# The second part of split weights, made by an accumulating DMA in place of a VectorE subtraction

## The chip, the cores and the metric

The kernel runs on one core of a Trainium2 chip. The metric is the device time of one execution in microseconds (us). A core has TensorE (PE in the profile, with its weight loads as PEld), VectorE (DVE), ScalarE (ACT), GpSimd (POOL), the SyncE queue (SP), and 16 DMA engines that move data for every queue that issues a DMA.

## The reference

Two layers of a diffusion backbone over 256 latent tokens `x` and 256 context tokens `ctx`, of 1024 channels each, all in float32. In each layer the same weights serve both streams:

```python
for layer in range(DEPTH):                       # DEPTH = 2
    x = x + 0.5 * mx[2] * swiglu(modulate(rms_norm(x), mx[0], mx[1]), ffn1_w_gu[layer], ffn1_w_down[layer])
    ctx = ctx + ...                              # the same, with mc and the same weights
    hx = modulate(rms_norm(x), mx[3], mx[4])     # attention, pooling and Fourier groups from hx @ w_in
    x = x + mx[5] * merge_mixers(...)            # ... @ w_out
    x = x + 0.5 * mx[8] * swiglu(modulate(rms_norm(x), mx[6], mx[7]), ffn2_w_gu[layer], ffn2_w_down[layer])
    if not last:                                 # ctx goes through mixer and second block in layer 0 alone
        ctx = ctx + ...
return rms_norm(x) * final_gain
# swiglu: g, u = split(h @ w_gu); (silu(g) * u) @ w_down, with 2816 hidden channels
# mx, mc = silu(c) @ ada_w[layer] + ada_b[layer], in nine parts of 1024
```

## The kernel before

Every large product is made exact to float32 by splitting both operands in two float32r parts, a rounded one and the rest. `mm3` then issues three matmuls for each 128 by 128 piece of a weight: rounded by rounded (L394), rounded weight by rest of the activation (L395), rest of the weight by rounded activation (L396). The input projection of the mixer does the same in L926 to L928.

The weights come through a `Feeder`. It holds a fixed plan: blocks of 1 MB in the order of their use, each loaded by one DMA of the SP queue (L160; the output projection's blocks by three) into one of three `raw` buffers. A block is used in two halves of 128 by 1024 values (512 KB), 300 halves in all. `split()` writes the rounded part of a half with ScalarE (L193), into a fresh tile `a`. `flush()` then writes the rest into a second tile with VectorE: `raw` minus rounded (L171). When both halves of a block have been flushed, its raw buffer is given back and `load()` issues the next block's DMA. So the DMA of block n+3 waits for the second subtraction of block n.

All of this is one straight program. `Sched` adds up an estimate of TensorE's time while the program is written, and side work is put between the matmuls when that estimate reaches its due time: `tick()` calls `split()` at least 1500 ns after the last one and `flush()` 1100 ns after its copy, unless the plan is held (`hold`) or six to eight halves (`limit`; two in attention) are split and not yet used up. `get()` splits at once where a half is needed and isn't there. The queues of the engines are in order, so what the program writes is what each engine does, and only its waits depend on time.

Two other streams share the queues. `ada_stream` loads the modulation weights in blocks of 512 KB by the SP queue (L568) and multiplies them on VectorE (L589, L591). The residual is updated on VectorE (L704), and gates and products of the feed-forward run on ScalarE (L662, L669) and VectorE (L667, L672). GpSimd has a memset of a small tile in each layer (L808) and no DMA.

In the first feed-forward blocks and layer 0 both streams go through the matmuls together (512 columns); the last feed-forward block, from about 1435 us on, has the latent stream alone (256 columns), so that each half of a weight serves half as much TensorE work.

Of the kernel before, what the change touches and what calls it, by code (L numbers as in the profile page):

```python
# [10 lines left out]
F32 = mybir.dt.float32  # L11
# [36 lines left out]

# Constants that depend on the shapes alone.
def _tables():  # L50
# [34 lines left out]
class Sched:  # L85
    """Places side work among the tensor engine's main stream by an estimate of its time."""

# [43 lines left out]
class Feeder:  # L131
    """Streams weight blocks in the order of their use and splits them into two exact float32r parts."""

# [32 lines left out]
    def flush(self):  # L166
        if self.part is None:
            return
        b, key, vh, vl, src = self.part
        self.part = None  # L170
        self.nc.vector.tensor_sub(vl, src, vh.bitcast(F32))  # L171
        self.live[key] = (vh, vl)
        b["left"] -= 1
        if b["left"] == 0:
            del self.raw[b["name"]]
            self.raw_live -= 1
            self.load()

    def split(self):
        self.flush()  # L180
        self.load()
        if self.n_split >= len(self.plan) or self.half_live >= self.limit:
            return False
        name, h = self.plan[self.n_split]
        if name not in self.raw:
            return False
        b = self.blocks[self.index[name]]
        src = b["halves"][h](self.raw[name])
        i = self.n_split
        view = (lambda t: t.rearrange("p (a b) -> p a b", a=src.shape[1])) if len(src.shape) == 3 else (lambda t: t[:, :])  # L190
        vh = view(self.tile(F32R))
        vl = view(self.tile(F32R))
        self.nc.scalar.copy(vh, src)  # L193
        self.part = (b, (name, h), vh, vl, src)
        self.half_live += 1
        self.n_split += 1
        self.next = self.S.t + SPLIT_GAP
        return True
# [31 lines left out]
def tile_hybrid_dit(  # L230
# [39 lines left out]

# [1 line left out]
    small = cst.tile([P, 802], F32, name="small", tag="small")  # L272
# [22 lines left out]

# [1 line left out]
    first_raw = {}  # L297
# [90 lines left out]

# [1 line left out]
    def mod(l, m, d, s):  # L390
# [10 lines left out]

# [1 line left out]
    def load_rows(l):  # L403
# [114 lines left out]

# [1 line left out]
    ada_ok = set()  # L520
# [10 lines left out]
    def ada_start(p):  # L531
        """Shift and scale of the first block for the channels p * 256 ..., on the tensor engine."""
        ps = psum()
        for m in range(2):
            for k in range(KD):
                raw = first_raw[p, m, k // 4][:, k % 4, :]
                j = k % 4
                mm(  # L538
                    ps[32 * j:32 * j + 32, m * 256:(m + 1) * 256], c32[:, k, :], raw,
                    start=(k < 4), stop=(k >= 4),  # L540
                )
            S.pe(900)
        sbt = t2()
        nc.vector.tensor_copy(sbt, ps)
        yield 600
        tp = psum()
        for i in range(4):
            mm(tp[:, 2 * i:2 * i + 2], sbt[:, i * P:(i + 1) * P], sel, start=True, stop=True)
        S.pe(1600)
        for m in range(2):  # L550
            c0 = m * 8 + p * 2
            nc.vector.tensor_tensor(
                out=modT[0][:, c0:c0 + 2, :], in0=tp[:, 4 * m:4 * m + 4].rearrange("p (i s) -> p i s", i=2),
                in1=vecT[0][:, c0:c0 + 2].unsqueeze(2).to_broadcast([P, 2, 2]), op=ALU.add,
            )
            mod_fix(0, m, c0, c0 + 2)
        ada_ok.add((0, "start", p))
# [82 lines left out]

# [1 line left out]
    def ffn(l, w, streams, h_tasks, tail, early=None):  # L642
# [142 lines left out]
    class Tail:  # L785
        """Collects squares of the new residual and starts the next normalization."""

# [13 lines left out]

# [1 line left out]
    def load_mix_consts(l):  # L803
# [16 lines left out]
    def qk_norm(src, nh, which, T):  # L820
        """RMS-norms the heads in src [128 tokens, nh, 64] (PSUM), with gain and rope; returns float32."""
        sq = t2()
# [32 lines left out]
    def mix(l, h_tasks, tail):  # L855
# [98 lines left out]

        # pooling and Fourier groups, the tensor engine's work between the steps of attention
        def pool_fft():
# [38 lines left out]
            def do_f2(s, _):  # L995
                # The real part for the frequencies 129 .. 255 mirrors that of 127 .. 1.
                ps = psum()
# [74 lines left out]

        # attention
        def attend(Ts, k0, nkc, per_unit, fill_ns):
# [93 lines left out]

        # output projection
        need_ada(l, 5)  # L1170
# [34 lines left out]

# [1 line left out]
    rows0 = load_rows(0)  # L1207
# [123 lines left out]

# [1 line left out]
    class End:  # L1333
# [76 lines left out]
```

## Time and profile before

| | |
|---|---|
| device time, median of two runs | 1625.3 us (1624.01 and 1626.58) |
| span of the profiled execution, first to last instruction | 1621.4 us, 3.9 us under that median |
| TensorE busy | 1599.8 us, 99% |
| VectorE busy | 1147.4 us, 71% |
| ScalarE busy | 589.5 us, 36% |
| GpSimd busy | 0.8 us |
| DMA engines' mean busy share, SP's queue | 44.5% |

Busy times are of one profiled execution, of which the profile gives the span and no other time of its own. An engine's share is over the whole span; the stages differ, and a table by stage stands among the rows below. A DMA packet's time counts on the one of the 16 engines that moves it, so a share of 44.5% is the mean over the 16.

### The profile page before, as it was taken

What the parts mean: (1) busy time and instruction counts of PE and PEld (TensorE: products, weight loads), DVE (VectorE), ACT (ScalarE), POOL (GpSimd) and SP (SyncE); (2) the same over time, 40 slices, a digit from 0 to 9 for tenths busy, and PEclk for the clock granted to TensorE, in tenths of its full rate; (3) what the DMA queues carried; (4) which work ended last, traced back from release to release, by engine and by line L of the source; (5) the groups of instructions that cost most, each with busy time, mean ns of one, the idle gap of its engine ahead of it and who ended that gap; (6) DMA issues with size and microseconds to landing.
All of it is one profiled execution on the core that took longest, in us unless ns stands there. A gap on an engine that the chain in (4) does not pass through costs nothing.

```text
span 1621.4 us, 22361 instructions
## 1 busy us (share of the span) xinstructions
PE 1599.8 (99%) x9039; PEld 1362.1 (84%) x9039; DVE 1147.4 (71%) x1959; ACT 589.5 (36%) x963; POOL 0.8 (0%) x6
## 2 busy tenths in 40 slices
PE   7999999999999999999999999999999999999998
PEld 5888888888886998888888898888888897899998
DVE  4788888886857567656644677888887587665556
ACT  4422232133557442222222352222232356654343
POOL 0000000000000000000000000000000000000000
PEclk9999999999999999999999999999999999999999
DMA  9756465553022335434432324555464323445452
GB/s 331 241 190 198 152 222 194 171 193 104 33 53 53 130 108 180 151 130 153 144 107 83 125 100 162 183 192 193 145 221 144 113 88 79 131 156 182 157 184 77
DMA packets 165590, 241.28 MB, mean 149 GB/s; under 512 B 6468, under 2 KB 115696, under 8 KB 165232
## 3 DMA queue, kind: packets, MB, share of 16 engines
q1 hardware_dynamic: 163536, 238.99, 44.5%
q8 instruction: 71, 1.16, 0.3%
q10 hardware_dynamic: 1952, 0.87, 0.2%
q14 instruction: 31, 0.25, 0.0%
HBM read 238.79 MB, written 1.05 MB: 148 GB/s over the span
## 4 chain that ended last, share of the span: by engine, by line
PE 97%; DVE 2%; ACT 1%; DMA 0%; issue 0%; SPq 0%; DVEq 0%
PE ps L394 28%; PE ps L395 28%; PE ps L396 27%; PE ps L926 2%; PE ps L928 2%; PE ps L927 2%; PE ps L1136 1%; PE ps L1113 1%; PE ps L603 1%; PE ps L1085 0%; PE ps L538 0%; PE ps L474 0%; PE ps L610 0%; PE ps L1086 0%; PE ps L484 0%; PE ps L902 0%
## 5 line engine op out<-in xcount | busy, mean ns | idle before, releaser
L394 PE MATMUL ps<-ahi,a 128*128 128x512 f32 (+1 forms) x1664 | 581.7, 350 | 1.7 <-ACT ahi L494 1.1
L395 PE MATMUL ps<-alo,a 128*128 128x512 f32 (+1 forms) x1664 | 578.4, 348 | 1.3 <-DVE alo L498 1.3
L396 PE MATMUL ps<-ahi,a 128*128 128x512 f32 (+1 forms) x1664 | 577.9, 347 | 1.5 <-DVE a L171 1.5
L171 DVE TENSOR_TENSOR a<-raw,a 128x1024 fp32r<-128x1024 f32 x300 | 363.5, 1222 | 138.2 <-ACT a L193 137.7
L394 PEld LDWEIGHTS ps<-ahi,a 128*128 128x128 f32 x1664 | 316.5, 190 | 51.5 <-issue 10.8
L193 ACT CAST a<-raw 128x1024 fp32r<-128x1024 f32 x300 | 304.8, 1044 | 150.2 <-PE ps L395 94.3
L396 PEld LDWEIGHTS ps<-ahi,a 128*128 128x128 f32 x1664 | 316.5, 190 | 41.0 <-DVE a L171 1.9
L395 PEld LDWEIGHTS ps<-alo,a 128*128 128x128 f32 x1664 | 316.6, 190 | 40.7 <-DVE alo L498 2.7
L591 DVE SCALAR_TENSOR_TENSOR a<-ada,c,a 128x512 f32<-128x512 f32 x448 | 320.6, 746 | 21.8 <-DMA ada<-in_ada_w_dram 21.2
L394 PE MATMUL ps<-a,a 128*128 128x512 f32 (+1 forms) x800 | 273.8, 342 | 0.0
L396 PE MATMUL ps<-a,a 128*128 128x512 f32 (+1 forms) x800 | 272.3, 340 | 0.0
L395 PE MATMUL ps<-a,a 128*128 128x512 f32 (+1 forms) x800 | 272.2, 340 | 0.0
L704 DVE SCALAR_TENSOR_TENSOR xT<-ps,modT,xT 128x256 f32<-128x256 f32 x336 | 149.2, 479 | 78.9 <-PE ps L396 78.5
L394 PEld LDWEIGHTS ps<-a,a 128*128 128x128 f32 x800 | 151.7, 190 | 20.9 <-issue 4.2
L396 PEld LDWEIGHTS ps<-a,a 128*128 128x128 f32 x800 | 151.7, 190 | 17.0
L395 PEld LDWEIGHTS ps<-a,a 128*128 128x128 f32 x800 | 151.8, 190 | 16.6
L669 ACT CAST a<-t 128x512 fp32r<-128x512 f32 (+1 forms) x88 | 49.9, 568 | 304.7 <-DVE t L667 304.7
L662 ACT ACTIVATE t<-ps 128x512 f32<-128x512 f32 (+1 forms) x88 | 47.7, 545 | 263.6 <-PE ps L396 260.4
L667 DVE TENSOR_TENSOR t<-ps,t 128x512 f32<-128x512 f32 (+1 forms) x88 | 54.4, 621 | 65.9 <-PE ps L396 56.4
L672 DVE TENSOR_TENSOR a<-t,a 128x512 fp32r<-128x512 f32 (+1 forms) x88 | 54.7, 625 | 24.3 <-ACT a L669 22.5
L494 ACT ACTIVATE ahi<-t,modT 128x256 fp32r<-128x256 f32 x88 | 43.6, 508 | 56.9 <-DVE t L491 56.8
L926 PE MATMUL ps<-a,ahi 128*128 128x512 f32 (+1 forms) x160 | 56.6, 354 | 0.0
(143 smaller groups left out, 979.3 us busy)
## 6 DMA issues: line engine op xcount, KB each, us to landing
raw<-in_ffn_w_gu_dram SPq DMA_DIRECT2D x88, 1024.0 KB, 5.2
ada<-in_ada_w_dram SPq DMA_DIRECT2D x128, 512.0 KB, 5.2
raw<-in_ffn_w_down_dram SPq DMA_DIRECT2D x44, 1024.0 KB, 5.2
raw<-in_w_in_dram SPq DMA_DIRECT2D x10, 1024.0 KB, 5.1
a<-in_ada_w_dram SPq DMA_DIRECT2D x16, 512.0 KB, 9.7
raw<-in_w_out_dram SPq DMA_DIRECT2D x16, 256.0 KB, 4.2
raw<-in_w_out_dram SPq DMA_DIRECT2D x8, 512.0 KB, 4.8
raw<-tab_pool SPq DMA_DIRECT2D x2, 1024.0 KB, 5.0
```

The lines of the kernel that those rows point to most:

```text
L171: self.nc.vector.tensor_sub(vl, src, vh.bitcast(F32))
L193: self.nc.scalar.copy(vh, src)
L394: mm(ps, whi, mhi, start=start, stop=False)
L395: mm(ps, whi, mlo, start=False, stop=False)
L396: mm(ps, wlo, mhi, start=False, stop=stop)
L591: nc.vector.scalar_tensor_tensor(out=acc[:, s, :], in0=raw[:, kk, :], scalar=sc, in1=acc[:, s, :], op0=ALU.mult, op1=ALU.add,)
L662: nc.scalar.activation(out=sg[:, :n], in_=g[:, :n], func=AF.Silu)
L667: nc.vector.tensor_mul(a[:, :n], u[:, :n], sg[:, :n])
L669: nc.scalar.copy(at[:, 0:n], a[:, :n])
L672: nc.vector.tensor_sub(at[:, 512:512 + n], a[:, :n], at[:, 0:n].bitcast(F32))
L704: nc.vector.scalar_tensor_tensor(out=xs, in0=ps[:, q * 256:(q + 1) * 256], scalar=mod(l, m0 + 2, d, s), in1=xs, op0=ALU.mult, op1=ALU.add,)
L926: mm(o, ph, whi[:, k, :wn], start=(kk == 0), stop=False)
```

## The change

`flush()` no longer subtracts on VectorE. `split()` makes ScalarE write the second tile too: the same half times -1, rounded to float32r, which is the negated rounded part. `flush()` then issues from GpSimd's queue a DMA that adds the raw half to that tile in place. Each half thus has one ScalarE operation more and one DMA from SBUF to SBUF of 512 KB, and one VectorE operation less. The rest of the diff removes comments.

```diff
@@ -168,7 +168,7 @@ def flush(self):
             return
         b, key, vh, vl, src = self.part
         self.part = None
-        self.nc.vector.tensor_sub(vl, src, vh.bitcast(F32))
+        self.nc.gpsimd.dma_start(out=vl, in_=src, accum_op=ALU.add)
         self.live[key] = (vh, vl)
         b["left"] -= 1
         if b["left"] == 0:
@@ -191,6 +191,7 @@ def split(self):
         vh = view(self.tile(F32R))
         vl = view(self.tile(F32R))
         self.nc.scalar.copy(vh, src)
+        self.nc.scalar.mul(vl, src, -1.0)
         self.part = (b, (name, h), vh, vl, src)
         self.half_live += 1
         self.n_split += 1
```

The instructions that move stand at one place of the last feed-forward block, around two blocks of gate and up weights (`raw` tiles), first ScalarE's queue in the kernel before, where `t` is a gate's output:

```order
L193 CAST a_2035_13013<-raw_12786 128x1024
L193 CAST a_2037_13032<-raw_12786 128x1024
L662 ACTIVATE t_2039_13041<-ps_13009 128x256
L193 CAST a_2041_13056<-raw_12841 128x1024
L193 CAST a_2043_13075<-raw_12841 128x1024
L662 ACTIVATE t_2045_13078<-ps_13043 128x256
```

and ScalarE's queue after the change, at the same two blocks (their buffers have other numbers, and lines after 193 are one higher):

```order
L193 CAST a_2035_13277<-raw_13046 128x1024
L194 ACTIVATE a_2036_13278<-raw_13046 128x1024
L193 CAST a_2037_13297<-raw_13046 128x1024
L194 ACTIVATE a_2038_13298<-raw_13046 128x1024
L663 ACTIVATE t_2039_13307<-ps_13273 128x256
L193 CAST a_2041_13322<-raw_13103 128x1024
L194 ACTIVATE a_2042_13323<-raw_13103 128x1024
L193 CAST a_2043_13342<-raw_13103 128x1024
L194 ACTIVATE a_2044_13343<-raw_13103 128x1024
L663 ACTIVATE t_2045_13346<-ps_13309 128x256
```

The negated copy stands right behind each rounded copy, ahead of the gate that follows. VectorE's queue before, at the same two blocks, held the four subtractions behind residual updates (`xT`) of the down projection:

```order
L704 SCALAR_TENSOR_TENSOR xT<-ps_12981,modT_74,xT 128x256
L704 SCALAR_TENSOR_TENSOR xT<-ps_12995,modT_74,xT 128x256
L171 TENSOR_TENSOR a_2036_13014<-raw_12786,a_2035_13013 128x1024
L171 TENSOR_TENSOR a_2038_13033<-raw_12786,a_2037_13032 128x1024
L171 TENSOR_TENSOR a_2042_13057<-raw_12841,a_2041_13056 128x1024
L171 TENSOR_TENSOR a_2044_13076<-raw_12841,a_2043_13075 128x1024
L667 TENSOR_TENSOR t_2049_13111<-ps_13080,t_2039_13041 128x256
```

and GpSimd's queue after the change holds these in their place, with nothing between them (what a row waits for in brackets: `DMASW` are DMAs of GpSimd's queue, `DMAHW` those of SP's and ScalarE's):

```order
L171 DMA a_2036_13278<-raw_13046 128x8x128 [waits DMAHW2_49,DMASW0_49,Activation_49]
L171 DMA a_2038_13298<-raw_13046 128x8x128 [waits DMASW1_49,Activation_49]
L171 DMA a_2042_13323<-raw_13103 128x8x128 [waits DMASW2_49,DVE_49,DMAHW3_49,PE_49,Activation_49]
L171 DMA a_2044_13343<-raw_13103 128x8x128 [waits DMASW3_49,PE_49,Activation_49]
```

So the second part no longer stands behind residual updates, but in a queue of its own. Last, SP's queue, which loads the raw blocks there, before the change:

```order
L160 DMA raw_12740<-in_ffn_w_gu_dram 128x8x256 [waits DMAHW6_49,DVE_49]
L160 DMA raw_12786<-in_ffn_w_gu_dram 128x8x256 [waits DMAHW7_49,DVE_49]
L160 DMA raw_12841<-in_ffn_w_gu_dram 128x8x256 [waits DMAHW0_49,DVE_49]
L160 DMA raw_12913<-in_ffn_w_gu_dram 128x8x256 [waits DMAHW1_49,DVE_49]
L160 DMA raw_13051<-in_ffn_w_down_dram 128x2x1024 [waits DMAHW2_49,DVE_49]
```

and after it:

```order
L160 DMA raw_12998<-in_ffn_w_gu_dram 128x8x256 [waits DMASW1_49,DMAHW6_49,DMASW0_49,Activation_49]
L160 DMA raw_13046<-in_ffn_w_gu_dram 128x8x256 [waits DMASW3_49,DMAHW7_49,DMASW2_49,Activation_49]
L160 DMA raw_13103<-in_ffn_w_gu_dram 128x8x256 [waits DMASW5_49,DMAHW0_49,DMASW4_49,Activation_49]
L160 DMA raw_13177<-in_ffn_w_gu_dram 128x8x256 [waits DMASW7_49,DMAHW1_49,DMASW6_49,Activation_49]
L160 DMA raw_13317<-in_ffn_w_down_dram 128x2x1024 [waits DMASW1_49,DMAHW2_49,DMASW0_49,Activation_49]
```

The order of the loads is as it was; each now waits for the two accumulating DMAs that read its buffer before, where it waited for a subtraction.

## Rows read from the trace of the kernel before

**Rows 1.** The page's head and its part 1, the busy time of each engine.

```profile
span 1621.4 us, 22361 instructions
...
PE 1599.8 (99%) x9039; PEld 1362.1 (84%) x9039; DVE 1147.4 (71%) x1959; ACT 589.5 (36%) x963; POOL 0.8 (0%) x6
```

**Rows 2.** The page's part 4, the chain that ended last, shares by engine.

```profile
PE 97%; DVE 2%; ACT 1%; DMA 0%; issue 0%; SPq 0%; DVEq 0%
```

**Rows 3.** The source view of line 171, the subtraction, with who waited for it.

```profile
L171 DVE TENSOR_TENSOR a<-raw,a x300: 1204/1222/1228, 22.4 to 1599.4; 128x1024 fp32r<-128x1024 f32 x150
...
  PEld ps L396: 1.9, 2
  PE ps L396: 1.5, 2
```

**Rows 4.** The page's part 5, the two operations of a split.

```profile
L171 DVE TENSOR_TENSOR a<-raw,a 128x1024 fp32r<-128x1024 f32 x300 | 363.5, 1222 | 138.2 <-ACT a L193 137.7
...
L193 ACT CAST a<-raw 128x1024 fp32r<-128x1024 f32 x300 | 304.8, 1044 | 150.2 <-PE ps L395 94.3
```

**Rows 5.** The page's parts 3 and 6, DMA queues and issues.

```profile
q1 hardware_dynamic: 163536, 238.99, 44.5%
...
raw<-in_ffn_w_gu_dram SPq DMA_DIRECT2D x88, 1024.0 KB, 5.2
ada<-in_ada_w_dram SPq DMA_DIRECT2D x128, 512.0 KB, 5.2
```

**Rows 6.** Windows by stage: us, busy by engine (count), clock, DMA share, GB/s.

```profile
0.00:60.00 60.00, 50.89 (x405) 41.19 (x405) 30.51 (x70) 25.34 (x43) 0.52 (x5) 0.97 0.89 290
60.00:380.00 320.00, 320.00 (x1446) 258.29 (x1445) 267.24 (x417) 86.72 (x109) 0.00 (x0) 1.00 0.57 189
380.00:590.00 210.00, 209.69 (x1370) 179.80 (x1369) 143.60 (x325) 113.79 (x258) 0.31 (x1) 1.00 0.22 67
590.00:960.00 370.00, 369.50 (x1837) 311.27 (x1836) 228.96 (x365) 109.22 (x151) 0.00 (x0) 1.00 0.38 129
960.00:1320.00 360.00, 360.00 (x1746) 298.07 (x1746) 278.18 (x438) 103.71 (x140) 0.00 (x0) 1.00 0.50 167
1320.00:1435.00 115.00, 108.97 (x739) 92.91 (x738) 85.92 (x185) 73.17 (x153) 0.00 (x0) 0.97 0.36 108
1435.00:1610.00 175.00, 175.00 (x1460) 175.00 (x1460) 108.22 (x154) 74.78 (x107) 0.00 (x0) 1.00 0.48 160
```

**Rows 7.** The same windows, VectorE's subtractions of line 171 alone.

```profile
0.00:60.00 60.00, 6.98 (x6) 0.97 0.89 290
60.00:380.00 320.00, 72.33 (x60) 1.00 0.57 189
380.00:590.00 210.00, 28.93 (x25) 1.00 0.22 67
590.00:960.00 370.00, 79.55 (x66) 1.00 0.38 129
960.00:1320.00 360.00, 79.07 (x66) 1.00 0.50 167
1320.00:1435.00 115.00, 26.48 (x22) 0.97 0.36 108
1435.00:1610.00 175.00, 70.12 (x58) 1.00 0.48 160
```

**Rows 8.** The source view of line 160: SP's DMA issue, ns min/median/max.

```profile
L160 SPq DMA_DIRECT2D raw<-in_ffn_w_gu_dram x88: 367/368/3880, 8.5 to 1564.6; - x88
...
L160 SPq DMA_DIRECT2D raw<-in_w_out_dram x24: 592/605/707, 457.7 to 1363.3; - x24
```

**Rows 9.** The timeline near 23 us, start and duration in us.

```profile
22.41 1.23 DVE L171 TENSOR_TENSOR a<-raw,a 128x1024 fp32r<-128x1024 f32 x1 [0.45 <-ACT a L193]
...
23.70 0.39 PE L396 MATMUL ps<-ahi,a 128*128 128x256 f32 x1 [0.76 <-DVE a L171]
```

**Rows 10.** Waits of SP's queue: us in total, times, longest.

```profile
SPq L160 <- DVE a L171: 752.2, 118, 37.2
```

## The prediction

> **What bounds the kernel now.** The head of the page and its first part come first: TensorE is busy 1599.8 of 1621.4 us [rows 1], and the chain that ended last lies on it for 97% [rows 2]. Whatever the change takes from VectorE can give back at most the 21.6 us in which TensorE stands idle, 1.3%. The source view of the subtraction then says how much of that idle time it causes: TensorE's matmuls waited for it for 1.5 us and its weight loads for 1.9 us, in two places each [rows 3]. So the step that is removed, though it is VectorE's costliest group at 363.5 us [rows 4], lies beside other work almost everywhere, and a gain of over 2% (32.5 us of 1625.3, about what a measurement of this kernel can tell from no change) is excluded. The question is what the new step costs, and on what.
>
> The windows by stage answer that [rows 6]. After the stretch each row has TensorE, its weight loads, VectorE, ScalarE and GpSimd, each in us with its count, then TensorE's clock, the DMA engines' busy share and GB/s. Five of the seven stages have a TensorE that is practically never idle, at full clock (1.00, the level of 2.4 GHz), and DMA engines that are busy for 22% to 57%. The first stage has 0.89 at 290 GB/s: there the DMA engines are nearly full already. The same windows for the subtraction alone count the halves that are split in each stage [rows 7]: 6, 60, 25, 66, 66, 22 and 58, which is 303, since three lie across a border.
>
> **What is removed.** 300 subtractions of 1.22 us on VectorE [rows 4], worth the few us above. The raw buffers were given back by them: SP's loads waited 752.2 us for a subtraction, 118 times [rows 10], so the next load starts as soon as the second half of a block is done. Whatever takes the subtraction's place sets the time of the next load too.
>
> **What is added on ScalarE.** 300 negated copies of the shape of the rounded copy, 1.04 us each [rows 4]: 313 us, which makes it 589 + 313 = 902 us of 1621, 56%. The last stage is the tightest: 74.8 us busy in 175 [rows 6], and 58 x 1.04 = 60.6 more makes 135, 77%. The in-order queue has room everywhere. Behind each negated copy stand gates and further splits, which come 1.04 us later and were not waited for by TensorE before. I cost it at nothing, except as part of the path below.
>
> **What is added on the DMA engines.** 300 transfers that read 512 KB of raw weights and 512 KB of the tile, and write 512 KB. No row shows an accumulating transfer or one inside SBUF. The nearest are the weight loads of SP's queue: 238.99 MB took 44.5% of the 16 engines' time [rows 5], which is 721.5 us for all 16, or 331 GB/s. At that rate 512 KB (0.524 MB), read once and written once, take 1.58 us of all engines. That is the lower bound, if the second read costs nothing. An addition in place needs two reads for each write, so I take two passes, 3.17 us. The upper bound is three passes, one for each read and one for the write, 4.75 us.
>
> The Trainium skill (Collectives: The Full Stack, section "The bandwidth ceiling: the fold count and why AG ≠ RS ≠ AR") states that an addition in the DMA engines is slowed not by the add but by its two source reads, which go through the same queue of read descriptors and halve the rate. By that rule the price is the two passes; by the loads' row alone, one read and one write, it is half of it, and the total is that of the first rival below. No run here shows it yet.
>
> **The sum by stage.** What a stage has left is its length times the idle share of its DMA engines [rows 6]; what is asked is its halves [rows 7] times 3.17 us. 0 to 60 us: 6.6 us left, 6 halves ask 19.0, 12.4 too many. 60 to 380: 137.6 left, 60 halves ask 190.2, 52.6 too many. 380 to 590: 163.8 left, 79 asked, fits. 590 to 960: 229.4 left, 209 asked, fits. 960 to 1320: 180 left, 209.2 asked, 29.2 too many. 1320 to 1435: 73.6 left, 69.7 asked, fits closely. 1435 to 1610: 91.0 left, 58 halves ask 183.9, 92.9 too many. The last stage is the worst because one stream alone gives each half 175 / 58 = 3.0 us of TensorE work, where the stage from 60 us gives 5.3. The excess is 187 us. It can't be carried into an idle stage: three raw buffers and a limit of six to eight halves keep the stream no more than about six halves of 5.3 us, 32 us, ahead. TensorE then waits in L396 or L928 for the second parts, and that is the time added.
>
> **The path of one half.** A half's second part was ready 1.22 us after its rounded copy. Now there are a negated copy of 1.04 us and a DMA; loads of 512 KB and 1 MB alike land 5.2 us after issue [rows 5], so I take 5.2, and the path grows by 1.04 + 5.2 - 1.22 = 5.0 us. Where halves are split well ahead this is hidden by the matmuls of the halves before; where a half is used at once it shows. The timeline near 23 us has such a place: L396 starts at 23.70 us, just behind the subtraction that began at 22.41 [rows 9]. That lies in a stage whose excess is counted. I add it once, for the stage from 1320 us, which has 4 us to spare: 5 us.
>
> For the raw buffers of the last stage the path matters too: load 5.2, a pace of 3.0 to the second half, two copies 2.1, DMA 5.2 make 15.5 us, where three buffers of two halves allow 18.1. That holds with free DMA engines; with full ones no buffer comes back in time, which is the same excess seen from SP's queue: L160 waits for the accumulating DMAs, and the modulation loads of L568 wait behind it.
>
> Span 1621.4 + 187 + 5 = 1813; with the 3.9 us by which the median of the runs stands above the profiled span, 1817, so I say **1820 us**, 12% slower. Within this case the least is a perfect spread of all transfers: 721.5 + 300 x 3.17 = 1673 us of DMA work, 1677 in all. The most comes if full DMA engines reach only the 0.89 of the first stage [rows 6]: asked and own work over 0.89 exceeds the stages by 21, 99, 0, 23, 77, 10 and 126 us, 356 in all, and with the path and the 3.9 us that is 1986.
>
> **Rivals.** First, **the transfers are hidden**, and the time is not slower by 2%. That needs an accumulating half at 1.58 us, as a load costs. Then the first stage is over by 2.9 us and the last by 0.8, and all others fit; the path of 5.0 us shows at the start and at perhaps three restarts of the stream after a hold, four times 5.0 or 20 us. 1621.4 + 3.7 + 20 + 3.9 = 1649. For it: most stages are far from full [rows 6]. Against it: the doubled reads. It decides up to 91 / 58 = 1.57 us for each half in the last stage, and above that each us more costs 58 us there.
>
> Second, **a dearer addition**: three passes, 4.75 us. The excess by stage is 21.9, 147.4, 0, 84.1, 133.5, 30.9 and 184.5 us, 602 in all, so 2227. Against it: the packets of the loads read and write at the same time, or 331 GB/s would not be reached. For it: a half of gate or up weights is cut into rows of 128 values, smaller pieces than a load's rows of 256.
>
> Third, **GpSimd's queue is the bound**: it must start 300 transfers one behind the other. No DMA of its queue is in the trace; SP's issue of a load takes 0.37 us, or 0.6 for the loads of the output projection [rows 8]. It decides from 3.0 us for each half in the last stage and 5.3 in that from 60 us. At 6 us the stages get longer by 173, 40, 26 (590 to 960), 36 and 17 us, 292 in all, so about 1917. Five to ten times the price of the nearest rows is needed, hence a small chance.
>
> Fourth, **the freed VectorE helps**: with 363.5 us less to do, residual updates and modulation come earlier. At the very best all 21.6 us of idle TensorE vanish: 1604, and that is still within 2%.
>
> **How the numbers follow.** Two passes and full DMA engines 0.47 (1677 to 1986), hidden 0.25 (1630 with no restart that shows, to 1690 with ten), three passes 0.16 (around 2227, or beyond), GpSimd's queue 0.11 (about 1917, open above), a freed VectorE 0.01. Within 2% means under 1658 us, and over 1593. About three fifths of the hidden case lie there, 0.15, and with the last case that is 0.16; none goes below 1593, and 0.01 is left for what I haven't seen. Slower by over 2%: 0.83. The range reaches from 1650, which leaves out less than half of the hidden case, to 2230, which leaves out half of the three passes: about 0.2 in all. The likeliest case's own range is 1677 to 1986.
>
> **What would show it.** In the profile after, a queue of GpSimd should take about 300 x 3.17 / 1820 = 52% of the 16 engines beside some 40% of SP's; the windows should have the DMA engines near 0.9 in the first two and the last stage, with TensorE below its full time there, at a clock that may fall below 1.00 where it starves; L396 should wait for DMAs of L171, most after 1435 us; L160 should wait for them too. VectorE should lose 363 us and ScalarE gain about 313. The hidden case shows a GpSimd queue at half that share and a TensorE at 98%. If the added packets take over 4 us for each half, the second rival holds; if the DMA engines are half idle in the last stage while TensorE waits, it is GpSimd's queue or the length of the path. What would make all of this wrong is a price outside 1.58 to 4.75 us for each half, since the sum is nearly proportional to it.

## The result, and the profile after

The changed kernel takes **2022.27 us** (median of two runs, 2021.22 and 2023.32) where the kernel before takes 1625.3: a ratio of 1.2443, 95% interval 1.2407 to 1.2479, slower. The profiled execution of after took 2021.22 us, with a span of 2019.4. The forecast was 1820 us, so +195 was expected and +397 came: the direction was right, the size was half.

The page of the changed kernel: its head, parts 1 and 3 (queue, packets, MB, share of the 16 engines), 4, 5 and 6. Lines behind 193 are one higher than before.

```profile
span 2019.4 us, 23411 instructions
...
PE 1710.4 (85%) x9039; PEld 1421.8 (70%) x9039; DVE 797.8 (40%) x1659; ACT 868.4 (43%) x1263; POOL 393.1 (19%) x306
...
q0 software_dynamic: 215232, 157.31, 58.5%
q1 hardware_dynamic: 163536, 238.99, 36.0%
...
PE 33%; DMA 29%; issue 26%; DVE 4%; POOL 4%; ACT 3%; SPq 1%; POOLq 0%; DVEq 0%; ACTq 0%
...
L194 ACT ACTIVATE a<-raw 128x1024 fp32r<-128x1024 f32 x300 | 316.6, 1055 | 13.6 <-PE ps L396 13.6
...
a<-raw POOLq DMA_DIRECT2D x300, 512.0 KB, 9.5
raw<-in_ffn_w_gu_dram SPq DMA_DIRECT2D x88, 1024.0 KB, 9.1
ada<-in_ada_w_dram SPq DMA_DIRECT2D x128, 512.0 KB, 8.3
```

TensorE's share of the chain fell from 97% [rows 2] to 33%, and 29% is now DMA. TensorE was idle for 21.6 us before [rows 1] and is for 309 now. The other 110 us of the loss are matmuls that run longer: its busy time rose from 1599.8 to 1710.4 us for the same 9039 matmuls. GpSimd's queue takes 58.5% of the 16 engines, where the forecast said 52%, and SP's 36.0%: together 94.5% over the whole span (a share, not a rate; the last section says why). A load of a gate and up block lands 9.1 us after its issue, where it was 5.2 [rows 5].

The windows of the changed kernel, cut where TensorE has got as far as in the stages of [rows 6] (the counts of its matmuls show it); the columns are those of [rows 6].

```profile
0.00:80.00 80.00, 52.32 (x407) 43.03 (x408) 24.71 (x66) 30.46 (x49) 9.65 (x10) 0.83 0.91 248
80.00:533.00 453.00, 351.49 (x1443) 270.66 (x1442) 198.16 (x356) 142.28 (x169) 78.03 (x60) 0.89 0.93 203
533.00:758.00 225.00, 215.14 (x1370) 183.48 (x1369) 116.62 (x299) 134.11 (x280) 28.21 (x24) 0.98 0.60 116
758.00:1154.00 396.00, 378.75 (x1836) 314.68 (x1835) 150.51 (x299) 171.79 (x217) 87.76 (x67) 0.97 1.03 208
1154.00:1579.00 425.00, 381.85 (x1745) 305.05 (x1745) 201.26 (x372) 165.74 (x206) 84.61 (x66) 0.94 1.02 223
1579.00:1721.00 142.00, 116.77 (x739) 98.90 (x738) 61.03 (x163) 92.80 (x176) 29.97 (x22) 0.90 0.84 151
1721.00:2009.00 288.00, 209.41 (x1472) 201.60 (x1471) 41.47 (x99) 128.73 (x166) 74.88 (x58) 0.86 1.12 212
```

The first column of lengths against [rows 6] gives the loss by stage: 20, 133, 15, 26, 65, 27 and 113 us. The forecast had 12, 53, 0, 0, 29, 5 and 93. The worst miss is the second stage, from 60 us before: 80 us more than the sum said. There the DMA share is 0.93, not the highest of the rows. Three stages that the sum said fit lose 15, 26 and 22 us more than it gave them, and one of them, the fourth, has a DMA share of 1.03. The granted clock, 1.00 (the level of 2.4 GHz) in five of the seven stages before, is 0.83 to 0.98: it is lowest where TensorE is idle for the largest share of the window, 0.83 in the first and 0.86 in the last. In the last, 1472 matmuls take 209.41 us of TensorE, where 1460 took 175.00 at 1.00.

Whom TensorE waits for, and SP's queue (us in total, times, longest), in the changed kernel:

```profile
PE ps L397 <- DMA a<-raw: 145.6, 56, 13.2
PE ps L604 <- DVE a L592: 111.2, 13, 20.3
...
ACT a L670 <- DVE t L668: 439.2, 64, 22.2
DVE a L592 <- DMA ada<-in_ada_w_dram: 374.7, 64, 18.4
...
SPq L160 <- DMA a<-raw: 1431.3, 140, 35.9
```

and in the kernel before:

```profile
ACT a L669 <- DVE t L667: 304.7, 84, 8.1
...
DVE a L591 <- DMA ada<-in_ada_w_dram: 21.2, 22, 2.1
```

The first wait was forecast: the matmul of the second part waits for the accumulating transfer. The second wasn't. L604 is the matmul of the modulation; it waits for VectorE's L592, which waits for a modulation load, and this load stands on SP's queue behind L160, which now waits 1431 us for transfers where it waited 752.2 for subtractions [rows 10]. VectorE's wait for these loads rose from 21.2 to 374.7 us. Of the 111.2 us, 71.3 lie in the window 80 to 533 us, the one that the sum missed most; of the 145.6 us there, 3.6.

The chain of the changed kernel shows one such wait (start, duration, what), its longest:

```profile
311.01 0.86 POOL a L171
311.87 5.78 issue
317.66 4.52 DMA a<-raw
...
322.32 0.37 SPq L160
...
322.78 10.91 DMA ada<-in_ada_w_dram
...
333.78 2.09 DVE a L592 x3
...
335.91 2.58 PE ps L604 x4
```

The transfer issued at 317.66 us lands at 322.2, and only then does SP start the next raw load, at 322.32. The modulation load behind it in the queue has had to stand there, starts at 322.78, takes 10.91 us beside everything else that moves, and TensorE, idle since 315.6, goes on at 335.91. Neither the transfer nor the raw load was what TensorE needed.

The 5.78 us before the transfer are no work of GpSimd: it waits there for ScalarE's negated copy. ScalarE was late because its queue stood at a gate (L670) until 314.85 us, for a product of VectorE (L668), and VectorE's queue had stood before that product for 2.63 us at an earlier modulation load (L592). So a late load delays the copies, the copies the transfers, and the transfers the next load. Over the kernel ScalarE's wait at this place rose from 304.7 to 439.2 us.

### The profile page after: what moved, and what is told of

Read it like the earlier page. It is cut to its first block, busy times and chain, and to the rows that moved or that the text cites. A ratio compares the mean times of both kernels' runs of the same rounds, so it can differ in the third digit from the quotient of the medians.

```text
span 2019.4 us, 23411 instructions
## 1 busy us (share of the span) xinstructions
PE 1710.4 (85%) x9039; PEld 1421.8 (70%) x9039; DVE 797.8 (40%) x1659; ACT 868.4 (43%) x1263; POOL 393.1 (19%) x306
## 3 DMA queue, kind: packets, MB, share of 16 engines
q0 software_dynamic: 215232, 157.31, 58.5%
## 4 chain that ended last, share of the span: by engine, by line
PE 33%; DMA 29%; issue 26%; DVE 4%; POOL 4%; ACT 3%; SPq 1%; POOLq 0%; DVEq 0%; ACTq 0%
DMA a<-raw 15%; PE ps L397 8%; PE ps L395 8%; PE ps L396 8%; DMA ada<-in_ada_w_dram 6%; DMA raw<-in_ffn_w_down_dram 4%; POOL a L171 4%; DMA raw<-in_ffn_w_gu_dram 3%; DVE a L592 1%; ACT a L193 1%; ACT a L194 1%; PE ps L929 1%; PE ps L927 1%; PE ps L928 1%; PE ps L604 1%
## 5 line engine op out<-in xcount | busy, mean ns | idle before, releaser
L171 POOL DMA_DIRECT2D a<-raw x300 | 392.3, 1308 | 1601.6 <-ACT a L194 1284.8
L397 PE MATMUL ps<-ahi,a 128*128 128x512 f32 (+1 forms) x1664 | 596.4, 358 | 87.4 <-DMA a<-raw 87.4
L395 PE MATMUL ps<-ahi,a 128*128 128x512 f32 (+1 forms) x1664 | 598.1, 359 | 1.7 <-ACT ahi L495 1.1
L396 PE MATMUL ps<-alo,a 128*128 128x512 f32 (+1 forms) x1664 | 593.2, 356 | 0.5 <-DVE alo L499 0.5
L592 DVE SCALAR_TENSOR_TENSOR a<-ada,c,a 128x512 f32<-128x512 f32 x448 | 314.7, 746 | 374.7 <-DMA ada<-in_ada_w_dram 374.7
L193 ACT CAST a<-raw 128x1024 fp32r<-128x1024 f32 x300 | 311.9, 1040 | 285.1 <-DMA raw<-in_ffn_w_gu_dram 119.5
L397 PEld LDWEIGHTS ps<-ahi,a 128*128 128x128 f32 x1664 | 330.2, 198 | 134.6 <-DMA a<-raw 94.8
L395 PEld LDWEIGHTS ps<-ahi,a 128*128 128x128 f32 x1664 | 330.5, 199 | 57.6 <-issue 14.1
L396 PEld LDWEIGHTS ps<-alo,a 128*128 128x128 f32 x1664 | 330.6, 199 | 40.1 <-DVE alo L499 1.3
L397 PE MATMUL ps<-a,a 128*128 128x512 f32 (+1 forms) x800 | 286.8, 358 | 58.5 <-DMA a<-raw 58.2
L194 ACT ACTIVATE a<-raw 128x1024 fp32r<-128x1024 f32 x300 | 316.6, 1055 | 13.6 <-PE ps L396 13.6
L395 PE MATMUL ps<-a,a 128*128 128x512 f32 (+1 forms) x800 | 285.1, 356 | 0.5 <-DVE xT L705 0.5
L396 PE MATMUL ps<-a,a 128*128 128x512 f32 (+1 forms) x800 | 282.7, 353 | 0.0
L670 ACT CAST a<-t 128x512 fp32r<-128x512 f32 (+1 forms) x88 | 49.5, 563 | 439.2 <-DVE t L668 439.2
L397 PEld LDWEIGHTS ps<-a,a 128*128 128x128 f32 x800 | 160.6, 201 | 85.1 <-DMA a<-raw 67.7
L395 PEld LDWEIGHTS ps<-a,a 128*128 128x128 f32 x800 | 161.4, 202 | 25.3 <-issue 4.2
L396 PEld LDWEIGHTS ps<-a,a 128*128 128x128 f32 x800 | 160.8, 201 | 17.7
L668 DVE TENSOR_TENSOR t<-ps,t 128x512 f32<-128x512 f32 (+1 forms) x88 | 54.2, 620 | 233.2 <-PE ps L397 157.0
L604 PE MATMUL ps<-a,small 128*32 128x512 f32 x128 | 50.0, 761 | 111.2 <-DVE a L592 111.2
```

Source lines behind the costliest of these rows:

```text
L171: self.nc.gpsimd.dma_start(out=vl, in_=src, accum_op=ALU.add)
L194: self.nc.scalar.mul(vl, src, -1.0)
L395: mm(ps, whi, mhi, start=start, stop=False)
L396: mm(ps, whi, mlo, start=False, stop=False)
L397: mm(ps, wlo, mhi, start=False, stop=stop)
L592: nc.vector.scalar_tensor_tensor(out=acc[:, s, :], in0=raw[:, kk, :], scalar=sc, in1=acc[:, s, :], op0=ALU.mult, op1=ALU.add,)
```

## The experiments

Each is one run beside a run of the kernel before (1624.2 to 1626.3 us). The theories go by letters: W, the work of the 16 DMA engines sets the time; L, R or P, the path of a second part through copy, GpSimd's issue and landing, with the raw buffers that come back late; G, GpSimd's queue; A, ScalarE's longer queue; Q, modulation loads that stand on SP's queue behind a raw load.

**ScalarE's part alone.** The negated copy stays, VectorE adds.

```diff
-        self.nc.gpsimd.dma_start(out=vl, in_=src, accum_op=ALU.add)
+        self.nc.vector.tensor_add(vl, vl.bitcast(F32), src)
```

> Only ScalarE's part of the change: the negated copy is made, and VectorE adds the raw half to it in place, with no DMA. If the DMA engines' work sets the time (theory W), 1625 us, within 10 of before, since nothing is added there. If ScalarE's longer queue (868 us busy instead of 590) has a part in it (theory A), 1660 or more.

Measured: 1637.44 us, 12 more than before. 300 operations of 1.06 us on ScalarE are nearly hidden, but not free, as the prediction had them: TensorE's mean granted clock is 0.993 (0.996 before) and its idle time is 10 us more. That is 2 us past what W allowed. Theory A, 1660 or more, falls; the other 385 us come with the DMA.

**A thin transfer.** An eighth of each half is added by the DMA (128 rows of 512 bytes), the rest by VectorE.

> All 300 accumulating DMAs, in the same places and with the same waits, but each adds an eighth of its half (128 rows of 512 B); VectorE adds the other seven eighths. Theory W: 8 packets of about 71 ns for each engine and half, 0.57 us, which fits in every stage: 1630 to 1660 us. If the path of a second part and the waits behind it set the time (theory L: a DMA takes microseconds to land however small, raw buffers come back late), or the 300 issues on GpSimd's queue (theory G), most of the loss stays: 1800 to 2000 us.

Measured: 1682.39 us, which is neither: W said 1660 at most, L and G 1800 at least. GpSimd's queue takes only 10.1% of the engines, and yet 45 us are lost beyond ScalarE's part. Something that goes with each transfer costs time while the engines are far from full.

**Plain copies.** The transfer copies and doesn't add.

```diff
-        self.nc.gpsimd.dma_start(out=vl, in_=src, accum_op=ALU.add)
+        self.nc.gpsimd.dma_start(out=vl.bitcast(F32), in_=src)
```

> The same 300 DMAs with the same bytes written, as plain copies: the tile is overwritten with the raw half, so the second part of each weight is not the rest but the half itself. One read instead of two. Theory W: packets at the price of a plain copy, about 27 ns for 512 B and 159 for 4096 B, 1.6 to 1.9 us for each half, excess 12 us, with the path some 1640 to 1670. Theory L and G: same landings and same issues, above 1900 us.

Measured: 1766.28 us, again between the two. GpSimd's queue takes 27.9%, 1.64 us per half, all engines some 70%. The step from copying to adding is worth 256 of the 397 us, and W alone (1670 at most) doesn't give the 141 that stay.

**The price by itself.** Nothing of the reference is computed: 32 transfers of 512 KB each, one behind the other on GpSimd's queue, added in rows of 512 bytes, added in rows of 4096, then copied in rows of 512, then in rows of 4096.

> No part of the reference's computation: 32 DMAs each of four forms from one SBUF tile to another, back to back from GpSimd's queue: accumulating with rows of 512 B, accumulating with rows of 4096 B, plain with rows of 512 B, plain with rows of 4096 B, each 512 KB. If the price is the operation's own: 65 ns and 328 ns for an accumulating packet, so a pace of 4.2 and 2.6 us for each DMA; plain 27 and 159 ns, 1.7 and 1.3 us. If the 3.94 us measured in the changed kernel come from contention with the weight loads, the accumulating packets alone cost twice the plain ones at most: 54 and 318 ns, 3.5 and 2.5 us.

Measured: 338.75 us. Its windows, one inside each of the four forms (us, VectorE and GpSimd busy, clock, DMA share, GB/s):

```profile
20.00:110.00 90.00, 0.00 (x0) 32.12 (x22) 1.00 1.29 136
170.00:215.00 45.00, 0.00 (x0) 14.70 (x17) 1.00 1.05 201
262.00:275.00 13.00, 0.00 (x0) 6.04 (x7) 1.00 0.95 263
290.00:320.00 30.00, 0.00 (x0) 12.20 (x23) 1.00 0.98 384
```

At these rates 0.524 MB take 3.86, 2.61, 1.99 and 1.37 us. An addition costs 1.93 and 1.91 times what a copy of the same rows costs, so two passes were right. The 3.86 us for short rows lie between the 4.2 and the 3.5 of the two readings in the expectation and settle neither; whether the loads beside them slow the additions further isn't shown. Of the 300 halves, 192 are cut in rows of 512 bytes and 108 in rows of 4096 (192 x 1024 + 108 x 128 packets and 16 small ones for each transfer make the 215232 of the page), 3.41 us at the mean.

**Long rows.** Gate and up blocks are loaded in two halves, each contiguous in the raw buffer.

```diff
-            name, [(lambda t: k3(t, 8), src)], None,
-            [lambda t, h=h: k3(t, 8)[:, :, h * P:(h + 1) * P] for h in range(2)],
+            name, [(lambda t, h=h: k3(t[:, h * 1024:(h + 1) * 1024], 8), src[:, :, h * P:(h + 1) * P]) for h in range(2)], None,
+            [lambda t, h=h: k3(t[:, h * 1024:(h + 1) * 1024], 8) for h in range(2)],
```

> The gate and up blocks are loaded as two transfers of 512-byte rows, so that each half lies contiguous and its accumulating transfer has 4096-byte rows; everything else as in the changed kernel. Prices of the run of single transfers: 2.63 us per half for all 300 instead of 3.86 for 192 of them; the loads of gate and up take some 60 us more of the 16 engines in all (27 ns per 512 bytes against 46 per 1024). Theory W (the DMA engines' work alone sets the time), stage by stage at 2.63 us: about 1740 us. Theory R (on top of the work, each block's raw buffer comes back only when its transfers have landed, so that loads can't run ahead and the swings within a stage are not evened out): W's 1740 and the 170 us that W leaves unexplained in the changed kernel, so 1860 to 1910. If the short rows do not matter: 2020.

Measured: 1926.5 us, 96 less than the changed kernel. The length of the rows counts. W alone (1740) is far off again, and R's 1860 to 1910 is missed by 16 us. The edit also cuts the loads of gate and up into rows of 512 bytes where they had 1024, and leaves the 16 halves of the output projection short, so the 96 us are the net gain.

**Every second half.** Odd halves by the DMA, even ones by VectorE's addition.

> Only every second half gets its second part by the accumulating transfer; the others by a VectorE addition onto the same negated copy. Theory W at the isolated prices: no stage but the first and the last is over its length, about 1640 to 1650 us. Theory R: between the run with thin transfers (1682, 0.57 us per half) and the run with plain copies (1766, 1.64 us per half); this one has 1.71 us per half on average, so about 1760 us.

Measured: 1750.54 us. W's 1640 to 1650 falls; the 1760 that theory R read off between two runs comes within 10 us. The odd halves are each block's first, so here SP's raw load never waits for a transfer that has just been issued, and SP's waits for transfers fall from 1431 to 1057 us: the run halves the work and eases SP's queue at once, and can't tell the two apart.

**A fourth raw buffer.** `RAW_BUFS = 4`, `TILE_BUFS = 20`.

> The changed kernel with 4 raw buffers in place of 3 (and 20 tile buffers in place of 22, to make room). Theory W: nothing changes, 2000 to 2030 us. Theory R: the fourth block lets loads start one block earlier; most of the 170 us that the engines' work leaves unexplained goes, 1850 to 1920 us.

Measured: 2033.29 us, 11 more. Theory R in this form falls: a further block, with two tile buffers fewer, doesn't help. The reason stands in the code: `flush()` calls `load()` right behind its transfer, so SP comes to the next raw load when that transfer has just been issued, however many buffers there are, and waits out its landing.

**The work without the wait.** The kernel before with its subtraction, and beside it one accumulating transfer for each half into one of two scratch halves that nobody reads (20 tile buffers, to make room).

```diff
         self.nc.vector.tensor_sub(vl, src, vh.bitcast(F32))
...
+        k = self.n_flush % 2
...
+            dst = self.scratch[:, k * 1024:(k + 1) * 1024]
...
+        self.nc.gpsimd.dma_start(out=dst, in_=vh.bitcast(F32), accum_op=ALU.add)
```

> The kernel before, its VectorE subtraction kept, and beside it one accumulating transfer per half from the first part's tile into a scratch buffer that nobody reads (20 tile buffers in place of 22): the DMA engines' work of the change without anybody waiting for it but the reuse of a tile much later. Theory W at isolated prices: the stages' excess alone, 1625 and some 225, so about 1850 us; by the changed kernel's whole time 1950 to 2020. Theory P (the loss is the path through the transfer, not the engines' work): 1630 to 1660 us.

Measured: 1913.76 us, +288, between W at the isolated prices (1850) and W by the changed kernel's whole time (1950). P falls: the engines' work costs most of the loss even where no matmul waits for its result. Three of its windows, at the places of the second, fifth and last stage:

```profile
67.00:469.00 402.00, 350.08 (x1444) 268.67 (x1443) 271.21 (x420) 85.74 (x109) 75.99 (x58) 0.93 1.02 224
...
1062.00:1465.00 403.00, 378.43 (x1742) 301.77 (x1741) 274.62 (x437) 102.57 (x140) 83.85 (x66) 0.97 1.07 235
...
1586.00:1895.00 309.00, 212.30 (x1460) 200.42 (x1460) 105.82 (x154) 75.81 (x106) 81.39 (x61) 0.80 1.09 197
```

The second stage loses 82 us here (133 in the changed kernel), the fifth 43 (65), the last 134 (113). In the last stage this run loses more than the changed kernel itself, so the 288 us are not a clean price of the work. Two things blur it: its transfers wait for one another in the two halves of the scratch buffer, and ScalarE at times waits for a tile that such a transfer still reads; TensorE waits 74.8 us in all for rounded copies (L202 of this run).

**A later load.** Four raw buffers, and a block's load issued one half later: the next `flush()` calls `pay()`.

```diff
+    def pay(self):
+        self.raw_live -= self.owed
+        self.owed = 0
+        self.load()
...
             del self.raw[b["name"]]
-            self.raw_live -= 1
-            self.load()
+            self.owed = 1
```

> The changed kernel with 4 raw buffers, and each block's load issued one half later, so that SyncE's queue doesn't stand at it until the transfer issued just before has landed. Theory Q (part of the loss is SyncE's queue: modulation loads stand behind a raw load that waits for a landing): TensorE's waits for the modulation matmuls shrink from 111 us to under 50, and the time falls by 50 to 110 from the 2033 us of the run with 4 raw buffers, to 1920 to 1980. Theory W (the DMA engines' work alone): 2010 to 2040.

Measured: 1961.08 us, 72 less than with four buffers alone. TensorE's waits in the modulation matmul fall to 40.3 us, from 93.5 with four buffers alone. Q holds.

**The same with plain copies.**

> The same edit on the kernel with plain copies (its second part is the raw half itself, so the computation is changed), where the DMA engines are some 70% full. It took 1766 us. Theory Q: most of its loss beyond the ScalarE copies' 12 us goes, 1650 to 1700. Theory W: 1750 to 1780, as the engines' work stays.

Measured: 1702.34 us, 64 less. Both miss: not most of the loss beyond ScalarE's part but half of it was SP's queue (if the fourth buffer gains nothing here either), and 65 us beyond that part stay.

**A queue of their own for the modulation loads.**

```diff
-                nc.sync.dma_start(
+                nc.scalar.dma_start(
```

> The changed kernel with the modulation loads issued on ScalarE's DMA queue, so that no raw load stands ahead of them; they now stand behind ScalarE's own work. Theory Q: 1900 to 1960. Theory W: 2000 to 2040. Above 2040 would say that ScalarE's order holds them up more than SyncE's did, and decides nothing.

Measured: 1928.61 us, 94 less than the changed kernel, from one word in a line that the change doesn't touch. TensorE's waits there:

```profile
PE ps L397 <- DMA a<-raw: 166.1, 56, 13.3
PE ps L604 <- DVE a L592: 16.9, 6, 4.6
```

The second is down from 111.2 us, the first, the wait for the second parts, isn't. SP's own wait for transfers even rose, from 1431 to 1715 us: what it costs depends on what stands behind it in the queue. ScalarE's wait for VectorE's product fell from 439.2 to 200.4 us. The stages of this run, cut at the same matmuls:

```profile
0.00:81.00 81.00, 53.30 (x408) 43.64 (x408) 24.69 (x66) 30.62 (x49) 9.65 (x10) 0.83 0.91 245
81.00:456.00 375.00, 340.31 (x1442) 266.31 (x1441) 199.92 (x355) 143.26 (x169) 77.50 (x60) 0.95 1.10 242
456.00:682.00 226.00, 214.61 (x1370) 182.60 (x1369) 116.88 (x300) 134.32 (x281) 28.08 (x23) 0.98 0.62 122
682.00:1077.00 395.00, 379.48 (x1835) 315.06 (x1834) 151.95 (x299) 171.40 (x216) 87.76 (x67) 0.97 1.03 209
1077.00:1477.00 400.00, 376.20 (x1750) 303.71 (x1749) 202.09 (x373) 166.93 (x208) 84.57 (x66) 0.97 1.08 237
1477.00:1623.00 146.00, 119.28 (x741) 101.03 (x740) 61.01 (x163) 93.22 (x176) 29.97 (x22) 0.88 0.84 149
1623.00:1915.00 292.00, 208.49 (x1454) 202.08 (x1454) 40.31 (x95) 127.70 (x164) 74.88 (x58) 0.84 1.10 208
```

The second stage takes 375 us and moves 242 GB/s, where it took 453 at 203. Against [rows 6] the stages lose 21, 55, 16, 25, 40, 31 and 117 us.

**Next to no work.** The thin transfer cut to 8 rows.

```diff
-        self.nc.gpsimd.dma_start(out=one(vl), in_=one(src), accum_op=ALU.add)
+        self.nc.gpsimd.dma_start(out=one(vl)[0:8], in_=one(src)[0:8], accum_op=ALU.add)
```

> The run with thin transfers, cut to 8 of their 128 rows: 4 KB per half, so next to no work for the DMA engines, but the same chain of ScalarE, GpSimd's issue, landing, and SyncE's wait. The other 120 rows of that eighth of a half don't get their addition, so the second part is wrong there. Thin took 1682 us. Theory P (the path through GpSimd and the landing costs by itself): 1665 to 1682. Theory W: 1637 to 1648, the time of the kernel with ScalarE's copy alone.

Measured: 1665.59 us. GpSimd's queue takes 1.1% of the engines, and 28 us are lost beyond ScalarE's part. This is what the path through a transfer costs with engines that have next to nothing to do for it, the waits of SP's queue included; P holds, at its lower edge.

**Both remedies of SP's queue.**

> Both remedies of SyncE's queue at once: modulation loads on ScalarE's queue, and 4 raw buffers with each load issued one half later. One alone took 2022 to 1929, the other 2033 to 1961. If both mend the same loss (modulation loads behind a waiting raw load): 1910 to 1930, and what is left is the DMA engines' work. If they mend two different losses: 1850 to 1870.

Measured: 1898.01 us, between the two. Of the later load's 72 us, 30 come on top of the own queue. Mostly it is one loss; what the 30 are is open.

**Long rows and the own queue.**

> Long rows for all accumulating transfers, and the modulation loads on ScalarE's queue. If the engines' work (price per half) and SyncE's queue are two separate parts of the loss, their gains of 96 and 94 us add up: 2022 less 190, about 1830 us (1815 to 1850). If they are the same loss, seen twice: 1900 to 1930.

Measured: 1834.11 us. The gains of 96 and 94 us add up to within 2: price and queue are two parts of the loss. It is the best version with 300 accumulating transfers of whole halves, and still 13% slower than the kernel before.

## Why the prediction was right in its direction and half too small

The direction, the bound and the two passes were right. 2022 us lies above the likeliest case's own range, 1677 to 1986; that the whole range, 1650 to 2230, holds it is luck, since its upper end was there for three passes, which did not come.

**What bounds the kernel, and what is removed:** right. VectorE lost 350 us of work (1147.4 to 797.8) and nothing came of it.

**ScalarE:** "I cost it at nothing, except as part of the path below" was 12 us too little by the run of ScalarE's part alone.

**The price of a transfer:** this is the first step that failed, in its size. "An addition in place needs two reads for each write, so I take two passes, 3.17 us": the run with the price alone shows two passes, at 3.41 us for the mean half. What was wrong is the base, the loads' 1.58 us: a copy in rows of 512 bytes takes 1.99. The prediction had seen the short rows ("smaller pieces than a load's rows of 256") and put them with the second rival, as if they belonged to three passes. At 3.41 us its own sum by stage gives 13.8, 66.8, 0, 0, 44.8, 1.3 and 106.6 us, 233 where it had 187: 46 of the shortfall.

The Trainium skill (Collectives: The Full Stack, section "The bandwidth ceiling: the fold count and why AG ≠ RS ≠ AR") says of the reduce step of a collective that the addition's two source reads halve its rate. The run with the price alone agrees: 136 against 263 and 201 against 384 GB/s.

**The sum by stage:** right in which stages are worst (the last and the second), wrong where it said "fits": the second step that failed. With the modulation loads on a queue of their own, the four stages that the sum called overfull (first, second, fifth and last) lose 21, 55, 40 and 117 us, 233 in all, and at 3.41 us the sum gives them 13.8, 66.8, 44.8 and 106.6, 232. The totals agree better than the stages do. The other three lose 16, 25 and 31 us, 72 in all, where the sum had the 5 us of the path. ScalarE's copies alone lengthen these three by 3, 0 and 7 us, the work without the wait by 0, 13 and 6, the path with next to no work, ScalarE's copies included, by 4, 0 and 6. None of them makes the 72, and the cause of the rest is open. That transfers which land late hold up a stream with three raw buffers, before a stage as a whole is full, is argued, not shown; the fourth buffer gave nothing. The plain copies with a later load tell no more: of the 65 us that they lose beyond ScalarE's part, the path with next to no work would make 28, the same rule some 7 at 1.64 us for each half (16 at 1.77, the mean by the rates of the run with the price alone), and the rest is open too.

**SP's queue:** the third step that failed, and the largest of them. The prediction named it and dismissed it in the same sentence: "which is the same excess seen from SP's queue: L160 waits for the accumulating DMAs, and the modulation loads of L568 wait behind it". It isn't the same excess. SP's queue stands still until a copy is made and its transfer has landed, and a modulation load behind it can be what TensorE needs next. That is a loss of 94 us with its own remedy, and it adds to that of the price. The path of 5.0 us, charged once, was too little as well: with next to no work on the engines it costs 28 us, and its term for the landing, 5.2 us, is 9.5 at the median in the changed kernel.

**The pieces together:** the span of 2019.4 us is 206 above the 1813 of the sum. The dearer transfer makes 46 of it and SP's queue 93 (2019.4 less the 1926.8 of the run with its own queue); the 67 that remain lie in the three stages that the sum said fit. That price and queue add up is shown by a run, long rows with the own queue; the 67 are what is left. The work without the wait and ScalarE's 12 us make 300, close to the 303 that the kernel with its queue mended loses, but that is an agreement of totals alone: the last stage has 134 there for 117, the fourth 13 for 25.

**The rivals:** hidden transfers fell (a DMA share above 0.9 in five of seven windows, TensorE 85% busy). Three passes fell by the price, 3.41 us for the mean half, under the 4 that was to be their sign. GpSimd's queue fell: an issue takes 0.86 to 2.10 us, 393 us in all, and GpSimd idles until ScalarE's copy for 1284.8 us. The freed VectorE showed nowhere.

**What would show it:** L397 waits for transfers most in the last stage, as said: 77.8 of its 145.6 us lie after 1721 us. GpSimd's queue came out at 58.5% instead of 52%; the clock fell in every stage, and the fourth and fifth stages have DMA shares of 1.03 and 1.02, not only those where it was looked for.

## What to carry to other kernels

Before an operation on an engine that isn't the bound becomes a DMA, ask which in-order queue will wait for its landing, and what stands behind that wait: here modulation loads that had nothing to do with the split cost 94 us. Price a transfer by the rows it is cut into, not by the rate of another queue's longer rows, and an accumulating one at twice a copy. And a stage that fits in a sum of work is not free: three such stages lost 72 us here, with SP's queue mended.

## What the hardware showed unexpectedly

- Added in rows of 512 bytes, 512 KB took 3.86 us, in rows of 4096 bytes 2.61. The 300 plain copies moved in 43200 packets over the whole kernel, the 300 additions in 215232, for the same rows and the same 157.31 MB.
- The DMA engines' busy share goes above 1: 1.29 with short accumulating rows alone, 1.12 in the last stage of the changed kernel. A share isn't a rate there: 58.5% of the span would be 3.94 us per half, where the rates give 3.41.
- GpSimd's issue of an accumulating transfer took 2.13 us in the run of the price alone for short rows and 0.88 for long ones; a plain one 0.89 and 0.53.
